# An rwkv7 and convolution block: the channel-tile loop ordered by a list scheduler, full-array chain products, the solve's small steps on GpSimd

## The chip, the cores and the metric

The kernel runs on one core of a Trainium2 chip. Its engines are TensorE (PE, with its weight loads PEld), VectorE (DVE), ScalarE (ACT), GpSimd (POOL) and SyncE (SP, which issues most DMAs). The metric is the device time of one execution in microseconds (us), as the median of three timed runs. A profile of one more execution gives the trace that all rows below come from.

## The reference

One block on 512 tokens and 1024 channels: an rwkv7 time mix and a conformer convolution run side by side on the normed input, are gated and merged, and a gated feed-forward part of width 2816 follows. What matters here is the loop over channel tiles:

```python
def wkv7(r, w, k, v, a, b):          # 16 heads of 64 channels
    def step(S, inp):
        r_t, w_t, k_t, v_t, a_t, b_t = inp
        sa = einsum('bhvk,bhk->bhv', S, a_t)
        S = S * w_t + sa[..., None] * b_t + v_t[..., None] * k_t
        return S, einsum('bhvk,bhk->bhv', S, r_t)
    ...
def conformer_conv(p_c, dw, ...):
    c = u * sigmoid(gate)             # u, gate = halves of p_c
    c = depthwise_conv(c, dw, 31 taps, causal) + dw_b
    return silu(layer_norm(c)) @ w_o
```

Before it stand r, k, v, the decay, a and g as products of the normed input with weights, partly through low-rank factors; behind it a norm per head, the gates and the output projections.

## The kernel before, in words

Channels lie on the partitions, tokens along the free dimension (T = 512). The loop runs over eight channel tiles of 128, that is two heads each. Every large fp32 product is made of three products of 128x512 with halves of the operands (hi by hi, hi by lo, lo by hi: `acc3`, L179 to L181). A weight arrives in fp32 (`wf`) and is split into `wh` and `wl`, by a copy on ScalarE and a subtraction on VectorE (L159, L160), or, for 106 halves inside the loop, by two copies on ScalarE (L168, L169) and an accumulating DMA of GpSimd's queue (L170).

Per tile, `plan_decay` makes the decay's exponentials and two low-rank products (`zw`, `za`, by `low2`, L412 and L413, the second of them over 64 rows); `plan_keys` and `plan_recept` make keys and receptance, each from a dense product `dn`; `plan_inner` makes the masked products inside chunks of 64 tokens (`gps`, L589) and writes the matrices `Mt`, `AR` and `GR`. `plan_solve` inverts (I - M): VectorE transposes `Mt` to `Mo` (L622), takes 31 steps of a product and a sum (`tt`, L634; `Ps`, L638), transposes back (`P`, L647), and small products (`wps` L659, `xps` L670) fill in the block matrix `Pbd`. `plan_values` makes the token-major values `UV` and `SV` (`vps` L695, `bps` L704). `plan_chain` is the recurrence over eight chunks: `zt` from `AR` and the state `SV` (L718), evicted as `zs` (L721), multiplied with `Pbd` (L726), evicted to `UV` (L738), then the state's update (L730 with the identity, L744 with `bkT`), evicted to `SV` (L751), and the outputs `yp` (L763, L759). All of these are 64-wide products, one for each of the two heads, on quarters or halves of the array. `plan_finish` norms the outputs; `plan_conv` runs the 31 taps of the convolution on VectorE (L841, L844).

The order of the program is a table of nominal times. Each piece is put down by `at(ct, t)`, where `ct` is the tile and `t` a position worked out from constants (PERIOD 44, SOLVE 25, CHP 5.5 and so on); at the end the list is sorted and called:

```python
    def at(ct, t):
        def add(fn):
            plan.append((ct * PERIOD + t, len(plan), fn))
...
    for t_, _, fn in sorted(plan, key=lambda e: e[:2]):
        fn()
```

Each engine takes its instructions in the order in which they are written, as far as their semaphores allow. Only taps and solve steps are tied to one another by hand (`order`, with `solved` and `tapped`), as both run on VectorE. Weights are loaded ahead as far as four buffers go (`plan_halves`).

## Time and profile before

| what | value |
| --- | --- |
| timed runs | 1147.42, 1139.44, 1155.11 us; median 1147.42 |
| profiled execution, span | 1165.1 us |
| mean granted TensorE clock over the span | 0.950 |
| busy share of PE, DVE, ACT, POOL | 98%, 62%, 53%, 8% |

The span goes from the first to the last instruction of the profiled execution, which is a little longer than the timed runs: the median of those is 0.985 of it. Sums of durations from the trace are made against the span. The loop of channel tiles lies between about 67 and 575 us, the taps of the last convolution tiles, the output projections and their norms behind it, and the feed-forward part runs from about 805 us to the end.

### The profile page before, as it was taken

To read this page: it belongs to the slowest core of one execution; us is meant where nothing else is said; L and a number is where in the kernel's file an instruction comes from. 1 tells how busy PE (TensorE), PEld (TensorE's weight loads), DVE (VectorE), ACT (ScalarE), POOL (GpSimd) and SP (SyncE) were. 2 spreads that over 40 slices of the span, in tenths; PEclk is the share of its full clock that TensorE was granted. 3 is DMA by queue.
4 is the path that set the end of the run, shared out by engine and by line. 5 is a ranking of instruction groups with operands and counts; after the bars stand their busy time and mean duration, and the time that the engine had idled before them with its cause. 6 is when DMAs were issued, how large, how long until landed. Compare 5 with 4: busy or idle time off the path is not lost.

```text
span 1165.1 us, 17942 instructions
## 1 busy us (share of the span) xinstructions
PE 1138.6 (98%) x6506; PEld 869.8 (75%) x6506; DVE 721.4 (62%) x1699; ACT 616.5 (53%) x1291; POOL 96.2 (8%) x140
## 2 busy tenths in 40 slices
PE   7999999999999999999999999999999999999996
PEld 5777675757676767677788788899888888888886
DVE  7968676747776748699698737546444444433324
ACT  6777776758756747564655724535333333333321
POOL 0111010101010101112222000000000000000000
PEclk9999988869988869899999999999999999999998
DMA  7145342524342423356798434500332322333322
GB/s 245 44 100 118 78 98 46 116 46 92 71 100 50 97 69 81 68 125 147 163 203 197 117 99 139 178 19 10 101 98 91 99 91 94 96 91 109 109 64 73
DMA packets 74202, 117.41 MB, mean 101 GB/s; under 512 B 15745, under 2 KB 21249, under 8 KB 74113
## 3 DMA queue, kind: packets, MB, share of 16 engines
q1 hardware_dynamic: 58848, 88.47, 25.2%
q0 software_dynamic: 15264, 27.79, 14.3%
q8 instruction: 51, 0.84, 0.3%
q14 instruction: 39, 0.31, 0.1%
HBM read 84.25 MB, written 2.10 MB: 74 GB/s over the span
## 4 chain that ended last, share of the span: by engine, by line
PE 91%; ACT 4%; DVE 3%; issue 1%; DMA 0%; SPq 0%; DVEq 0%; ACTq 0%
PE dn L179 22%; PE dn L181 22%; PE dn L180 22%; PE gps L589 3%; PE yp L759 2%; PE zt L726 2%; PE zt L718 2%; PE vps L695 1%; PE zt L744 1%; PE yp L763 1%; PE bps L704 1%; PE ss L194 1%; PE psf L180 1%; PE psf L179 1%; PE psf L181 1%
## 5 line engine op out<-in xcount | busy, mean ns | idle before, releaser
L159 ACT ACTIVATE wh<-wf 128x512 fp32r<-128x512 f32 (+1 forms) x172 | 106.6, 621 | 245.5 <-PE dn L180 237.8
L160 DVE TENSOR_TENSOR wl<-wf,wh 128x512 fp32r<-128x512 f32 (+1 forms) x172 | 116.0, 676 | 136.1 <-ACT wh L159 136.1
L179 PE MATMUL dn<-HH,wh 128*128 128x512 f32 x408 | 173.0, 426 | 0.8 <-DVE cpad L823 0.5
L844 DVE SCALAR_TENSOR_TENSOR ca<-cpad,dw,ca 128x512 f32<-128x512 f32 x240 | 171.8, 744 | 1.4
L180 PE MATMUL dn<-HL,wh 128*128 128x512 f32 x408 | 172.1, 422 | 0.0
L181 PE MATMUL dn<-HH,wl 128*128 128x512 f32 x408 | 171.1, 420 | 0.0
L170 POOL DMA_DIRECT2D wl<-wf x106 | 91.6, 870 | 505.3 <-ACT wl L169 325.6
L181 PE MATMUL dn<-FHH,wl 128*128 128x512 f32 x320 | 127.0, 397 | 0.0
L179 PE MATMUL dn<-FHH,wh 128*128 128x512 f32 x320 | 126.6, 395 | 0.0
L180 PE MATMUL dn<-FHL,wh 128*128 128x512 f32 x320 | 125.8, 393 | 0.0
L168 ACT ACTIVATE wh<-wf 128x512 fp32r<-128x512 f32 x106 | 66.3, 629 | 69.1 <-PE dn L180 68.1
L179 PEld LDWEIGHTS dn<-HH,wh 128*128 128x128 f32 x408 | 78.9, 194 | 18.9 <-issue 0.7
L181 PEld LDWEIGHTS dn<-HH,wl 128*128 128x128 f32 x408 | 78.6, 193 | 17.6 <-issue 0.5
L180 PEld LDWEIGHTS dn<-HL,wh 128*128 128x128 f32 x408 | 79.0, 194 | 16.4 <-issue 0.4
L180 PEld LDWEIGHTS dn<-FHL,wh 128*128 128x128 f32 x320 | 60.2, 188 | 15.0
L181 PEld LDWEIGHTS dn<-FHH,wl 128*128 128x128 f32 x320 | 60.1, 188 | 14.5
L179 PEld LDWEIGHTS dn<-FHH,wh 128*128 128x128 f32 x320 | 60.0, 188 | 13.8
L169 ACT ACTIVATE wl<-wh 128x512 fp32r<-128x512 f32 x106 | 66.3, 628 | 2.1 <-ACT UV L738 0.4
L179 PE MATMUL dn<-FH,wh 128*128 128x512 f32 (+1 forms) x166 | 64.3, 387 | 0.0
L181 PE MATMUL dn<-FH,wl 128*128 128x512 f32 (+1 forms) x166 | 64.1, 386 | 0.0
L180 PE MATMUL dn<-FH,wh 128*128 128x512 f32 (+1 forms) x166 | 64.1, 386 | 0.0
L638 DVE TENSOR_TENSOR Ps<-Ps,tt 128x60 f32<-128x60 f32 (+24 forms) x248 | 52.6, 212 | 3.4
(303 smaller groups left out, 2111.0 us busy)
## 6 DMA issues: line engine op xcount, KB each, us to landing
wf<-in_w_in_dram SPq DMA_DIRECT2D x112, 256.0 KB, 3.1
wl<-wf POOLq DMA_DIRECT2D x106, 256.0 KB, 3.7
wf<-in_w_gt_dram SPq DMA_DIRECT2D x44, 256.0 KB, 2.6
wf<-in_w_up_dram SPq DMA_DIRECT2D x44, 256.0 KB, 2.8
wf<-in_w_dn_dram SPq DMA_DIRECT2D x40, 256.0 KB, 2.7
wf<-in_w_ro_dram SPq DMA_DIRECT2D x16, 256.0 KB, 3.0
wf<-in_w_co_dram SPq DMA_DIRECT2D x16, 256.0 KB, 2.6
wf<-in_w_o_dram SPq DMA_DIRECT2D x16, 256.0 KB, 2.9
```

The costliest lines, as they stand in the source:

```text
L159: S.activation(out=hi, in_=src, func=AF.Copy)
L160: V.tensor_sub(lo, src, f(hi))
L168: S.activation(out=wh, in_=wf, func=AF.Copy)
L169: S.activation(out=wl, in_=f(wh), func=AF.Copy, scale=-1.0)
L170: G.dma_start(out=wl, in_=wf, accum_op=ALU.add)
L179: PE.matmul(ps, lhsT=a, rhs=rh(k), start=first and j == 0, stop=False)
L180: PE.matmul(ps, lhsT=a, rhs=rl(k), start=False, stop=False)
L181: PE.matmul(ps, lhsT=b, rhs=rh(k), start=False, stop=last and j == n - 1)
L589: PE.matmul(ps[:, c, :], lhsT=bk[R, hc * 4 + c, :], rhs=AR[R, hc * 4 + c, par:par + 2, :], start=True, stop=True)
L638: solved[0] = V.tensor_add(Ps[:, 0:j, q0:8], Ps[:, 0:j, q0:8], tt)
L718: PE.matmul(zt[R, 0, :], lhsT=AR[:, c, 2 * par, :], rhs=SV[:, c, par, :], start=True, stop=True)
L844: a_ = V.scalar_tensor_tensor(out=o_, in0=cb[:, j:j + T], scalar=tap(j), in1=o_, op0=ALU.mult, op1=ALU.add)
```

## The change

The table of nominal times goes. In its place each tile's work is written as generators (`prep`, `solve`, `values`, `chain`, `finish`, `taps`), whose calls go to a list scheduler in the source (`Sched`). It holds its own estimate of what every instruction takes (`times`), finds dependencies from the operands' regions, and at each turn takes, among the ready instructions that could start within EPS of the earliest, the one of the best priority: chain 0, loads and the low-rank inputs 1, `prep` and `values` 2, `solve` and `finish` 3, dense products 4, taps 5. Every engine's instructions are then pinned in that order, by a dependency on the last one issued. Lines of these instructions all read L290, the call inside the scheduler; only code outside it keeps its own lines.

Four other things change. The chain step's products become one each over the whole array: `AR` is stored so that both heads' parts stand side by side, `Pbd` is block diagonal and 128 wide, and the identity and `bkT` products take both heads in 128x128; `zs` is evicted in two instructions instead of one, and the outputs `yp` are made four chunks at a time (`outputs`). The second low-rank product takes all 128 rows, with a zero-padded `w2l`. The solve's 62 products and sums per tile go from VectorE (V) to GpSimd (G). The buffers of `Mt` go from 1 to 2, the taps add up in a buffer of their own (`cacc`), and 56 weight halves instead of 106 go through GpSimd's DMA, the others through VectorE's subtraction.

On PE, inside a chain step in the middle of a tile, this stood before (`dn` are dense products, `zt` and `yp` the chain's):

```order
L744 MATMUL zt<-UV,bkT 64x64 x2
L763 MATMUL yp<-GR,UV 64x64 x2
L181 MATMUL dn<-HH,wl 128x512
L179 MATMUL dn<-HH,wh 128x512
L759 MATMUL yp<-AR,SV 64x64
L180 MATMUL dn<-HL,wh 128x512
L718 MATMUL zt<-SV,AR 64x64 x2
L759 MATMUL yp<-AR,SV 64x64
L181 MATMUL dn<-HH,wl 128x512
L179 MATMUL dn<-HH,wh 128x512
L180 MATMUL dn<-HL,wh 128x512
L726 MATMUL zt<-zs,Pbd_484 64x64 x2
```

And now, again from one chain step to the next:

```order
L290 MATMUL zt<-zs,Pbd_513 128x64
L290 MATMUL dn<-HL,wh 128x512
L290 MATMUL dn<-HH,wl 128x512
L290 MATMUL dn<-HH,wh 128x512
L290 MATMUL dn<-HL,wh 128x512
L290 MATMUL zt<-SV,cs 128x128
L290 MATMUL zt<-UV,bkT 128x128
L290 MATMUL dn<-HH,wl 128x512
L290 MATMUL dn<-HH,wh 128x512
L290 MATMUL dn<-HL,wh 128x512
L290 MATMUL dn<-HH,wl 128x512
L290 MATMUL dn<-HH,wh 128x512
```

The pairs of 64x64 products have become single ones of 128x128 or 128x64, the `yp` are gone from between them, and dense products stand between every two.

On DVE, from the transpose `Mo` of one tile on, this stood before (`tt` and `Ps` are the solve, `ca` the taps):

```order
L622 STREAM_TRANSPOSE Mo<-Mt 128x1024
L634 TENSOR_TENSOR tt<-Mo,Ps 128x31
L638 TENSOR_TENSOR Ps<-Ps,tt 128x31
L634 TENSOR_TENSOR tt<-Mo,Ps 128x30
L638 TENSOR_TENSOR Ps<-Ps,tt 128x30
L634 TENSOR_TENSOR tt<-Mo,Ps 128x29
L705 TENSOR_TENSOR ya<-bps,mu_v 128x512
L638 TENSOR_TENSOR Ps<-Ps,tt 128x29
L495 SCALAR_TENSOR_TENSOR cum<-cs,cum 128x512
L634 TENSOR_TENSOR tt<-Mo,Ps 128x28
L531 TENSOR_SCALAR n_3380<-ss 128x8
L638 TENSOR_TENSOR Ps<-Ps,tt 128x28
```

Now the rows ahead of the transpose `P` of the third tile (number 2) are these, where `cacc` and `ca` are taps and products of the convolution:

```order
L290 SCALAR_TENSOR_TENSOR cacc<-ca,dw,cacc 128x512 x2
L290 SCALAR_TENSOR_TENSOR ca<-th,dn 128x512
L290 SCALAR_TENSOR_TENSOR cacc<-ca,dw,cacc 128x512 x2
L290 TENSOR_TENSOR g2l<-g2f,g2h 128x128
L290 SCALAR_TENSOR_TENSOR cacc<-ca,dw,cacc 128x512 x4
L290 SCALAR_TENSOR_TENSOR ca<-ca,dw,cacc 128x512
L290 TENSOR_SCALAR cacc<-ca,dw,pr 128x512
L290 SCALAR_TENSOR_TENSOR cacc<-ca,dw,cacc 128x512 x14
L290 SCALAR_TENSOR_TENSOR mu_v<-dn,pr,mu_v 128x511
L290 SCALAR_TENSOR_TENSOR cacc<-ca,dw,cacc 128x512 x3
L290 STREAM_TRANSPOSE P_1913<-Ps 128x32x8
L290 STREAM_TRANSPOSE P32T<-P_1913 128x256
```

The solve's steps have left VectorE, and taps stand in a row where they used to alternate with them.

On POOL, over some two tiles in the middle of the loop, this stood before (`wl` are the weight DMAs):

```order
L170 DMA wl<-wf 128x512 x6
L701 MEMSET SV 64x64
L702 MEMSET SV 64x64
L498 MEMSET ep 128x8
L170 DMA wl<-wf 128x512 x7
L701 MEMSET SV 64x64
L702 MEMSET SV 64x64
L170 DMA wl<-wf 128x512
L498 MEMSET ep 128x8
L170 DMA wl<-wf 128x512 x8
```

Now the first rows of the third tile's solve read:

```order
L290 DMA wl<-wf 128x512
L290 TENSOR_TENSOR tt<-Mo,Ps 128x31
L290 TENSOR_TENSOR Ps<-Ps,tt 128x31
L290 TENSOR_TENSOR tt<-Mo,Ps 128x30
L290 TENSOR_TENSOR Ps<-Ps,tt 128x30
L290 TENSOR_TENSOR tt<-Mo,Ps 128x29
L290 TENSOR_TENSOR Ps<-Ps,tt 128x29
L290 TENSOR_TENSOR tt<-Mo,Ps 128x28
L290 TENSOR_TENSOR Ps<-Ps,tt 128x28
L290 TENSOR_TENSOR tt<-Mo,Ps 128x54
L290 TENSOR_TENSOR Ps<-Ps,tt 128x27x2
L290 DMA wl<-wf 128x512
```

The solve's chain of products and sums is now GpSimd's, with weight DMAs between its steps, each of which waits for ScalarE's copy of the weight.

The diff, cut to its core ("..." marks what is left out; in the old code, `plan_solve` and `plan_chain` stand above):

```diff
-BUFS = (2, 2, 2, 2, 1, 1, 1)
-# nominal positions that order the program
-PERIOD = 44.0
-NCL = 3
-CPERIOD = 96.0
-CPERIOD2 = 20
-DTZ = 0.25
-CONV0 = 60
-TG_ = 25
+BUFS = (2, 2, 2, 2, 2, 1, 1)
+EPS = 0.15
 WBF = 4
-T0P = 0.0
-T1P = 475
-TE0 = -26.0
-TN0 = -10
-DTC = 0.3
-POST = 8
-TZO = 20
-LEAD = 11
-DTF = 0.9
-SOLVE = 25.0
-CH0 = -2
...
+        LAG = {"PE": 0.06, "ACT": 0.07, "DVE": 0.06, "POOL": 0.1, "SP": 0.1}
...
+            if eng == "PE":
+                lhsT, rhs = k["lhsT"], k["rhs"]
+                n, m = math.prod(rhs.shape[1:]), math.prod(lhsT.shape[1:])
+                if lhsT.dtype == F32R:
+                    c = max(0.112, 0.452e-3 * n)
+                elif name == "transpose":
+                    c = 0.112
+                elif m > 64:
+                    c = 2 * max(0.112, 1.02e-3 * n)
+                else:
+                    c = 0.058 if m > 32 else 0.016
+                return c, c + 0.17, 0.0
...
+            if eng == "POOL":
+                t = 0.2 + (1.0e-3 if len(aps) < 3 else 2.2e-3) * n
+                return t, t, 0.0
...
+        def after(self, d, o, kind):
+            if d.eng == o.eng and not d.land:
+                return 0.0 if kind == 1 or d.eng == "PE" else d.end + 0.03
+            return d.end + self.LAG[d.eng]
...
+        def issue(self, o, s):
+            e, t = o.eng, max(self.clock[o.eng], o.ready)
+            if o.mode is not None:
+                if self.mode not in (None, o.mode):
+                    t += 0.12
+                self.mode = o.mode
+            self.now = max(self.now, t)
+            self.clock[e] = t + o.busy
+            o.end = t + o.took
+            if o.land:
...
+            i = fn(*a, **k)
+            if self.last[e] is not None:
+                order(i, self.last[e])
+            self.last[e] = i
...
+        def feed(self):
+            self.loaded = [u for u in self.loaded if not u[-1].issued]
+            while len(self.loaded) < WB:
+                if not self.halves:
+                    i = next((i for i, e in enumerate(self.items)
+                              if all(n in self.posted for n in e[0])), None)
+                    if i is None:
+                        return
+                    self.halves += self.items.pop(i)[1]()
+                ld, units = self.halves.pop(0)
+                self.cur, self.pri = "load", 1
+                ld(G if self.fast else None)
+                self.cur, self.pri = "dense", 4
+                self.loaded.append([u() for u in units])
...
+                for e in self.ENGS:
+                    heads = [(max(self.clock[e], q[0].ready), q[0], s)
+                             for s, q in self.queues[e].items() if q and not q[0].wait]
+                    if not heads:
+                        continue
+                    t0 = min(h[0] for h in heads) + EPS
+                    t, o, s = min((h for h in heads if h[0] <= t0),
+                                  key=lambda h: (h[1].pri, h[1].seq))
+                    if best is None or t < best[0]:
+                        best = t, o, s
+                if best is None:
+                    break
+                _, o, s = best
+                self.queues[o.eng][s].pop(0)
+                self.issue(o, s)
...
+    V, G, S = Engine("DVE", nc.vector), Engine("POOL", nc.gpsimd), Engine("ACT", nc.scalar)
+    PE, SY = Engine("PE", nc.tensor), Engine("SP", nc.sync)
...
-    def low2(ps, h_, l_, R, X):
+    def low2(ps, h_, l_, X):
         PE.matmul(ps, lhsT=h_, rhs=X, start=True, stop=False)
-        PE.matmul(ps, lhsT=l_[R], rhs=X[R], start=False, stop=True)
+        PE.matmul(ps, lhsT=l_, rhs=X, start=False, stop=True)
...
+    def dense_tile(wap, then, rh=hh, rl=hl, need=(), ev=None):
...
+            if k == NT - 1:
+                sc.pri = 1
+                then(d["ps"])
+                sc.pri = 4
+                if ev:
+                    sc.post(ev)
...
+    def prep(ct):
...
+        for R, c in ((E, slice(0, P)), (O, slice(P, 2 * P))):
+            V.tensor_sub(w2l[R, c], w2f[R, c], f(w2h[R, c]))
...
+    def solve(ct):
         s_ = st[ct]
-
...
+        for j in range(B32 - 1, 0, -1):
             q0 = j // 4
             n = 8 - q0
             tt = kp.tile([P, j, n], F32, tag="tt", bufs=2, name="tt")
-            a_ = V.tensor_mul(tt, Mo[:, j, 0:j].unsqueeze(2).to_broadcast([P, j, n]),
-                              Ps[:, j, q0:8].unsqueeze(1).to_broadcast([P, j, n]))
-            if tapped[0] is not None:
...
-            solved[0] = V.tensor_add(Ps[:, 0:j, q0:8], Ps[:, 0:j, q0:8], tt)
...
+            G.tensor_mul(tt, Mo[:, j, 0:j].unsqueeze(2).to_broadcast([P, j, n]),
+                         Ps[:, j, q0:8].unsqueeze(1).to_broadcast([P, j, n]))
+            G.tensor_add(Ps[:, 0:j, q0:8], Ps[:, 0:j, q0:8], tt)
...
+        pb = Pbd[ct % 2]
+        for h in range(2):
+            for j, R in enumerate((R1[h], R2[h])):
+                S.activation(out=pb[R, :, h * L + j * B32:h * L + (j + 1) * B32], in_=P32[R],
+                             func=AF.Copy)
...
+    def chain(ct):
         s_ = st[ct]
...
+        if ct:
+            yield ("chain", ct - 1)
+        yield ("val", ct)
+        yield ("solve", ct)
+        AR, GR, UV, SV, pb, bkT, dL = (s_[n] for n in ("AR", "GR", "UV", "SV", "pb", "bkT", "dL"))
+        yp = None
+
+        def outputs(cs_):
+            for c in cs_:
+                if c > 0:
+                    for par, R in ((0, E), (1, O)):
+                        PE.matmul(yp[R, c, :], lhsT=SV[R, c, par, :], rhs=AR[R, c, 2, :],
+                                  start=c == 1, stop=False, skip_group_check=True)
+            for c in cs_:
+                for par, R in ((0, E), (1, O)):
+                    PE.matmul(yp[R, c, :], lhsT=UV[:, c, par, :], rhs=GR[:, c, par, :],
+                              start=False, stop=True, skip_group_check=True)
+
+        for c in range(NCH):
+            zt = pc.tile([P, 5, L], F32, tag="ch", name="zt")
+            PE.matmul(zt[:, 0:2, :], lhsT=AR[:, c, 0:2, :], rhs=SV[:, c, :, :],
+                      start=True, stop=True)
+            zs = sp.tile([P, L], F32, tag="zs", name="zs")
             for par, R in ((0, E), (1, O)):
...
+                S.activation(out=zs[R], in_=zt[R, par, :], func=AF.Copy)
+            PE.matmul(zt[:, 2, :], lhsT=pb[:, c, :], rhs=zs, start=True, stop=True)
             for par, R in ((0, E), (1, O)):
...
+                S.activation(out=UV[R, c, par, :], in_=zt[R, 2, :], func=AF.Copy)
             if c < NCH - 1:
+
+                if c > 0:
+                    PE.matmul(zt[:, 3:5, :], lhsT=ident, rhs=SV[:, c, :, :],
+                              start=True, stop=False)
+                PE.matmul(zt[:, 3:5, :], lhsT=bkT[:, c, :], rhs=UV[:, c, :, :],
+                          start=c == 0, stop=True)
                 for par, R in ((0, E), (1, O)):
...
+                    S.activation(out=SV[R, c + 1, par, :], in_=zt[R, 3 + par, :], func=AF.Identity,
                                  scale=dL[R, c:c + 1])
...
+            if c == NCH // 2 - 1:
+                yp = s_["yp"] = py.tile([P, NCH, L], F32, tag="y", name="yp")
+                outputs(range(0, NCH // 2))
+        outputs(range(NCH // 2, NCH))
+        sc.post(("chain", ct))
+        sc.spawn(once(lambda: finish(ct)), 3)
...
+    def taps(ct):
+        tap = lambda j: dw[:, ct * KW + j:ct * KW + j + 1]
+        yield ("cv", ct)
+        if ct:
+            yield ("taps", ct - 1)
         else:
...
+            yield "low1"
+        cb, o_ = conv_in[ct], csum_[:, 0:T]
+        V.tensor_scalar(out=o_, in0=cb[:, 0:T], scalar1=tap(0), scalar2=vec("conv_b", ct),
+                        op0=ALU.mult, op1=ALU.add)
+        for j in range(1, KW):
+            to = o_ if j < KW - 1 else conv_place(ct)[:, KW - 1:]
+            V.scalar_tensor_tensor(out=to, in0=cb[:, j:j + T], scalar=tap(j), in1=o_,
+                                   op0=ALU.mult, op1=ALU.add)
+        sc.post(("taps", ct))
+        if ct == NT - 1:
+            sc.fast = False
...
+        for g_, pri in ((prep, 2), (values, 2), (chain, 0), (taps, 5)):
+            sc.spawn(g_(ct), pri)
```

## Rows read from the trace of the kernel before

**Rows 1.** The page: busy us, share of the span; granted clock in 40 slices.

```profile
PE 1138.6 (98%) x6506; PEld 869.8 (75%) x6506; DVE 721.4 (62%) x1699; ACT 616.5 (53%) x1291; POOL 96.2 (8%) x140
PEclk9999988869988869899999999999999999999998
```

**Rows 2.** Table by stretches (from:to, length, then as its header says).

```profile
core 0: us, PE busy (x) PEld busy (x) DVE busy (x) ACT busy (x) POOL busy (x), PEclk, DMA share, GB/s
67.00:575.00 508.00, 501.44 (x3497) 345.12 (x3496) 357.91 (x1071) 337.39 (x819) 70.62 (x97) 0.89 0.41 89
223.00:286.00 63.00, 62.59 (x415) 41.35 (x415) 39.86 (x131) 41.02 (x101) 6.45 (x10) 0.78 0.32 70
286.00:337.00 51.00, 50.49 (x412) 35.15 (x411) 39.34 (x129) 39.32 (x98) 7.31 (x11) 1.00 0.42 91
...
900.00:1000.00 100.00, 100.00 (x431) 80.59 (x430) 48.06 (x72) 34.15 (x54) 0.00 (x0) 1.00 0.30 95
```

**Rows 3.** The same table for the dense products dn alone.

```profile
67.00:575.00 508.00, 291.50 (x959) 172.40 (x960) 19.77 (x27) 21.48 (x33) 0.89 0.41 89
...
286.00:337.00 51.00, 27.17 (x90) 15.47 (x90) 2.17 (x3) 1.96 (x3) 1.00 0.42 91
```

**Rows 4.** The same table, the loop's six stretches at half clock (one, and all).

```profile
225.40:252.70 27.30, 27.30 (x131) 16.18 (x132) 13.54 (x49) 13.24 (x37) 1.06 (x2) 0.51 0.20 39
...
sum 109.20, PE 109.06 PEld 67.58 DVE 47.91 ACT 54.71 POOL 6.01; mean PE 18.18 PEld 11.26 DVE 7.98 ACT 9.12 POOL 1.00
```

**Rows 5.** Chain of waits, 286 to 300 us: start, us, what.

```profile
289.49 0.86 PE vps L695 x6
290.35 0.27 PE zt L744 x4
290.62 0.12 PE yp L763 x4
...
291.38 0.26 PE yp L759 x2
291.64 0.27 PE zt L718 x4
...
293.00 0.26 PE zt L726 x4
293.27 0.12 PE zt L730 x4
293.38 0.42 PE za L413
...
298.62 0.43 PE dn L181
299.05 0.23 PE dn L179
```

**Rows 6.** By tile: duration ns min/median/max, first and last start.

```profile
L659 PE MATMUL wps<-P32T,Mt x256: 191/191/212, 106.3 to 510.6; 32*32 32x32 f32 x128
L638 DVE TENSOR_TENSOR Ps<-Ps,tt x248: 157/216/243, 80.7 to 506.7; 128x60 f32<-128x60 f32 x12, 128x54 f32<-128x54 f32 x8, 128x66 f32<-128x66 f32 x8, 128x28 f32<-128x28 f32 x8
L622 DVE STREAM_TRANSPOSE Mo<-Mt x8: 1908/1927/1965, 78.5 to 465.3; 128x1024 f32<-128x1024 f32 x8
```

**Rows 7.** GpSimd by line and shape: busy us, mean ns, idle before.

```profile
L170 POOL DMA_DIRECT2D wl<-wf x106 | 91.6, 870 | 505.3 <-ACT wl L169 325.6 <-DVE wg L160 53.3 <-ACT zs L721 21.8
L701 POOL MEMSET SV<- 64x64 f32 x8 | 1.5, 189 | 22.3 <-ACT zs L721 14.3 <-ACT wh L168 8.0
```

**Rows 8.** Chain of waits, 500 to 512 us, at a tile's transposes.

```profile
506.89 1.32 DVE ca L844 x2
508.22 0.62 DVE P L647
```

**Rows 9.** The page, and ScalarE by line: the weight halves.

```profile
L160 DVE TENSOR_TENSOR wl<-wf,wh 128x512 fp32r<-128x512 f32 (+1 forms) x172 | 116.0, 676 | 136.1 <-ACT wh L159 136.1
L169 ACT ACTIVATE wl<-wh 128x512 fp32r<-128x512 f32 x106 | 66.3, 628 | 2.1 <-ACT UV L738 0.4
```

More of the change, by code (lines that the diff above doesn't have):

```diff
@@ L810, in plan_conv, with conv_place, conv @@
+    conv_in = {}
+    def conv_place(ct):
+        if "ca" not in acts:
+            acts["ca"] = hp.tile([P, NT, KW - 1 + T], F32, tag="ca", name="ca")
+            G.memset(acts["ca"][:, :, 0:KW - 1], 0.0)
+        return acts["ca"][:, ct, :]
+    def conv(ct):
         cv = {}
-        t0 = conv_at(ct)
-        cb = cpad[ct % 2]
         def gate(ps):
@@ L886, in _ @@
         mid["YL"] = mp.tile([P, NT, T], F32R, tag="m2", name="YL")
+        sc.post("mid")
+        for m in range(NT):
+            yield ("ya", m)
+            split(act("ya")[:, m, :], mid["YH"][:, m, :], mid["YL"][:, m, :])
+        sc.post("split")
     def gate_c(m, ps):
```

948 lines of the change are left out of this document (517 added, 431 removed).

## The prediction

> **What bounds the kernel now.** The page comes first: TensorE is busy 98% of a span of 1165.1 us, VectorE 62%, ScalarE 53%, GpSimd 8% [rows 1]. A busy TensorE is not one at its peak, so the next view is the table by stretches. In the feed-forward part, 900 to 1000 us, 431 products of 128x512 take 100 us at full clock, 0.232 us each [rows 2]. That is the price of a dense product with nothing in its way, and the reader should hold the loop of channel tiles against it. The loop's body lies between 67 and 575 us: 508 us, of which the dense products are 959 [rows 2, 3]. At 0.232 they are worth 223 us, and 285 us remain, 35.7 us for each of the eight tiles. Tiles follow one another about every 58 us (the product wps, one group per tile, starts at 106.3 in the first and by 510.6 in the last [rows 6]). The stretch 286 to 337, one tile at full clock, takes 51 us with 90 dense products: 51 - 20.9 = 30.1 us beside them [rows 2, 3]. The stretch before it takes 63 us at clock 0.78. So what is to be had lies in the loop, in the 36 us per tile that are no dense products: 109.2 us of the loop pass at 1.2 GHz, in six stretches [rows 4], and within a chain step the change of shapes costs TensorE more than the arithmetic does [rows 5]. Behind 575 the dense products run nearly back to back, and the change leaves their number as it is; I cost that part at nothing.
>
> **Chain step (priced from the chain of waits at full clock).** Before, one step is seven groups of half-array products: zt L718 0.27, yp L763 0.12, yp L759 0.26 twice, zt L726 0.26, zt L730 0.12, zt L744 0.27, together 1.56 us. Each return to a dense product costs it 0.43 where its neighbours have 0.23 [rows 5], and a step has four returns: 1.56 + 4 x 0.19 = 2.32 us. After, a step has AR.SV, Pbd.zs, ident.SV and bkT.UV as one product each, 3.6 on average as the first and last chunk have fewer. Such a product of plain fp32 is in the trace as two passes; vps L695 has six passes of 128x128 in 0.86 us, 0.143 each [rows 5], so 0.29 a product and 1.05 a step. The four yp products of a step, batched four chunks at a time, cost what a group of four passes without a change of shape costs (0.12, zt L730), twice: 0.24. One change of shape per step is 0.26 - 0.12 = 0.14. Sum 1.43, saved 0.89 us in each of 64 steps: **-57 us**. The four evictions of a step become five (zs split in two), on a ScalarE that is 53% busy; they lie on the chain's own path, beside dense products. The second low-rank product goes from 64 rows to 128, so it no longer costs 0.42 (za L413) but 0.23, like any product of that size behind one of its own shape [rows 5]; two per tile and the returns with them: **-5 us**.
>
> **The order from a list scheduler.** By my working the best stretch pays 30.1 us beside the dense products and the average tile 35.7. The scheduler offers a dense product whenever a chain product waits, on every engine at once; I take it that all tiles then cost what the best one does: 8 x 5.6 = **-45 us**. Ends: nothing, if as much time at half clock comes back [rows 4], and about -60 if the best tile is beaten too. Against it stand 64 x 4 hand-offs between TensorE and ScalarE, now placed by a model of the times where they were placed by hand; I estimate 0.1 us each for what the model misses: **+25 us** (0 to 50; the nearest rows are the ends of a dense product, 0.23 us, which is what a late product costs in order).
>
> **The solve on GpSimd.** 62 small products and sums per tile leave VectorE, where they cost 0.21 us each [rows 6], about 100 us in all, and come to GpSimd. No row shows a two-input operation there. Nearest below: VectorE's own 0.21, and GpSimd's memset of 64 columns, 0.189, which reads nothing. Above: the issue of a weight DMA on GpSimd, 0.87 [rows 7]. I take 0.35, about two of the memsets, since it reads two operands and writes one. A tile's solve is then 62 x 0.35 = 21.7 us, plus seven weight DMAs that the order puts between its steps, 7 x 0.87 = 6.1, plus VectorE's transposes Mo 1.93 and P and P32T 0.62 each [rows 6, 8]: 31 us. Its cover is what TensorE has queued between the last masked product gps of a tile and its first wps, which waits for P. In tile 2 these are 93 dense products (21.6 us), 29 chain products (8.3), 30 yp and some norm products: about 34 us by the prices above. Counted the same way the eight tiles have 32.6, 37.9, 33.8, 35.0, 29.2, 34.0, 34.0 and 16.6. So the solve is just covered except in tile 4 (2 us) and the last (14): **+15 us**. What stands behind a late wps is everything on TensorE, since each engine's order is pinned: the dense products too. Each 0.1 us more per step is some 6.2 us per tile, 45 us in all; at VectorE's price the term is about 5, at the DMA's price over 200.
>
> **Costed at nothing.** 50 weight halves go from GpSimd's accumulating DMA to a subtraction on VectorE: 50 x 0.68 = 34 us more there and 50 x 0.63 less on ScalarE [rows 9], while VectorE loses the solve's 100 us; if its cover were gone, 34 us would show. The taps (0.66 us each back to back [rows 8]) all come before the last tile's solve in the new order, where they used to run on to 629 us; the layer norm behind them waits for the output products' turn in either. GpSimd's queue: a weight DMA now stands between solve steps and waits for ScalarE's copy; its buffer is one of four, so a wait of a microsecond holds a solve, which the 31 us above include only as the 0.87 of the issue.
>
> **Sum.** -57 - 5 - 45 + 25 + 15 = -67 us on a span of 1165.1, so 1098. The three timed runs have their median at 1147.42, 0.985 of the span. Forecast: 1098 x 0.985 = **1081 us**, -5.8%. The three runs spread over 1.4%, so about 2% is what a measurement can tell from no change.
>
> **Rivals.** *First, the taps hold the solve (slower).* VectorE and GpSimd now run two-input operations at the same time, which before never happened. The Trainium skill, "SBUF — State Buffer", section "Who interferes with whom", says that a VectorE instruction with two SBUF inputs contends with a GpSimd instruction that reads SBUF, and that the one that comes second is blocked wholly. No row here shows it, since GpSimd read nothing but in DMAs. As a mechanism of this kernel: the order puts 16, 34, 29, 25, 23, 25, 1 and 0 taps on VectorE between a tile's Mo and its P, 153 in all. If a solve step waits out a whole tap each time, 153 x 0.66 = 101 us come on top of solves that have no cover left. 1081 + 0.985 x 101 = **1180 us**. It decides the sign from about half of that wait: the forecast loses its lead of 66 us when a step's mean with its waits passes 0.35 + 66/440 = 0.50 us. For it: the taps stand back to back in those places, and nothing else on GpSimd's path has slack. Against it: only that no trace shows a block. *Second, GpSimd is slow by itself*, 0.6 us a step or more without any tap: + 0.25 x 450 = 113, **1190 us** and above. Memset rows speak against it, the DMA row for it. *Third, the order doesn't do what it says*: half clock stays (no -45, or hand-offs at the upper end): 1081 + 45, **about 1125 us**.
>
> **How the numbers follow.** Forecast with its own range 1040 to 1110: 0.50. Third rival 0.18, first 0.23, second 0.09. The low end is the sum without its two additions, 1165.1 - 107 = 1058, times 0.985: 1042. The upper end must take in most of the first rival: 1190. Faster by over 2% means below 1124.5: the forecast and half of the third with a little of a weak first: 0.62. Within 2%: 0.16. Slower: 0.22.
>
> **What the new profile would show.** Solve steps on GpSimd at 0.35 us start to start, and no longer beside taps than beside an idle VectorE (then the first rival is wrong). wps waiting for P under 3 us per tile but for the last. zt products of 128x128 at 0.29 us with no dense product of 0.43 behind them. Granted clock in the loop near 1. A wait of TensorE for P of 10 us and more in tiles 1 to 5, with taps running through it, is the first rival; the same with VectorE idle is the second. The prediction is wrong by its own terms if dense products beside the chain cost clearly over 0.232 us at full clock.

## The result, and the profile after

The changed kernel takes 1247.08 us (median of four runs, 1244.74 to 1253.8) against 1146.04 before (median of four too): a ratio of 1.0896, 95% interval 1.0821 to 1.0971. The forecast was 1081 with 1190 as its upper end; the sign is wrong, and only the second rival, "1190 us and above", reaches as far, whose condition (0.6 us a step without any tap) is not met below.

The profile of the kernel before (1165.1 us at a granted clock of 0.950) is of an execution some 20 us slower than the median of its timed runs, that of the changed kernel (1243.0 us) is not, so the two profiles differ by 78 us where the timed runs differ by 101.

The page of the changed kernel, answering to [rows 1]: TensorE is busy 90% instead of 98%, GpSimd 21% instead of 8%, and the granted clock is under 0.9 in 14 slices ahead of the last one, up to the 20th of 40, instead of 9.

```profile
PE 1123.8 (90%) x6042; PEld 900.1 (72%) x6042; DVE 709.6 (57%) x1261; ACT 615.8 (50%) x1311; POOL 257.9 (21%) x587
...
PEclk9879898979887887877699999999999999999998
```

The loop now ends near 640 us, where it ended near 575. The table by stretches of the changed kernel (columns as in [rows 2]), first everything, then the dense products alone as in [rows 3]:

```profile
67.00:350.00 283.00, 239.28 (x1407) 185.69 (x1408) 212.29 (x372) 177.10 (x407) 142.79 (x282) 0.88 0.40 87
350.00:640.00 290.00, 240.24 (x1613) 184.98 (x1613) 161.83 (x314) 171.78 (x462) 112.33 (x293) 0.80 0.21 53
```

```profile
67.00:350.00 283.00, 151.33 (x514) 98.51 (x515) 11.60 (x16) 10.95 (x17) 0.88 0.40 87
350.00:640.00 290.00, 120.19 (x373) 69.17 (x373) 8.82 (x12) 8.68 (x13) 0.80 0.21 53
```

573 us hold 887 dense products, where 508 us held 959 [rows 3]. That accounts for the whole difference between the two profiles: 65 us later, with 72 products of 0.232 us still to do, 17 us, makes 82, and the span is 78 us longer. TensorE is idle for 94 of these 573 us, where it was idle for 7 of the 508 [rows 2]. What TensorE waited for in the changed kernel (us in total, times, longest us):

```profile
PE wps L290 <- DVE P32T L290: 24.2, 6, 8.5
PE dn L290 <- DMA wl<-wf: 22.3, 11, 3.4
PE gps L290 <- ACT Mt L290: 8.9, 8, 4.3
```

The first is the solve coming late. The prediction allowed 2 us for it in tile 4 and 14 in the last; it came in tiles 1, 2, 4 and 5, with 4 to 8.5 us each, and with 0.4 in the last. Before, the same wait was this:

```profile
PE wps L659 <- DVE P32T L650: 0.9, 2, 0.5
```

The second is new and was not in the sum: dense products wait for weight halves whose DMA stands behind solve steps in GpSimd's queue. No such wait stands among those of the kernel before.

The solve's steps in the changed kernel, by tile, answering to [rows 6] (ns min/median/max), and its weight DMAs, answering to [rows 7]:

```profile
L290 POOL TENSOR_TENSOR tt<-Mo,Ps x248: 202/296/1082, 99.2 to 589.0; 128x60 f32<-128x60 f32 x12, 128x54 f32<-128x54 f32 x8, 128x66 f32<-128x66 f32 x8, 128x28 f32<-128x28 f32 x8
L290 POOL TENSOR_TENSOR Ps<-Ps,tt x248: 203/319/1562, 99.5 to 589.3; 128x60 f32<-128x60 f32 x12, 128x54 f32<-128x54 f32 x8, 128x66 f32<-128x66 f32 x8, 128x28 f32<-128x28 f32 x8
```

```profile
L290 POOL DMA_DIRECT2D wl<-wf x56 | 50.4, 914 | 103.8 <-ACT wl L290 69.1 <-PE tps L290 15.3 <-PE ss L290 9.7
```

A median of 0.3 us and a maximum of 1.56: the steps come in two kinds. Sorted by what VectorE does at the same time, 219 of the 496 lie beside an operation that reads two operands from SBUF and take 0.62 us on the mean (median 0.67), 226 lie beside nothing at 0.276, and 42 beside an operation with one operand in PSUM at 0.282. From the first step to the last, the solves of tiles 0 to 4 last 36 to 41 us, those of the last two, which have next to no taps beside them, 25 and 24. That is no longer than before, where steps alternated with taps on VectorE and the eight solves lasted 24 to 49 us by the same count: what is new is that TensorE waits for their end.

One place shows the two kinds of steps. Of the chain of waits from 107 us (start, us, what), and VectorE's own row of time beside it:

```profile
107.16 0.30 POOL tt L290
107.46 0.07 issue
107.53 0.88 POOL Ps L290
...
108.48 0.36 POOL tt L290
108.84 0.07 issue
108.91 0.73 POOL Ps L290
...
110.99 1.07 POOL Ps L290
```

```profile
107.53 0.69 DVE L290 TENSOR_TENSOR GL<-lo_f,GH 128x512 fp32r<-128x512 f32 x1 [5.69 <-ACT GH L290]
108.14 0.55 DVE L290 TENSOR_SCALAR cacc<-cpad,dw,pr 128x512 f32<-128x512 f32 x1
108.72 3.94 DVE L290 SCALAR_TENSOR_TENSOR cacc<-cpad,dw,cacc 128x512 f32<-128x512 f32 x5
```

The same `Ps` step that takes 0.3 us takes 0.88 when a two-operand subtraction of 0.69 starts with it, and 0.73 to 1.07 through the five taps.

### The profile page after: what moved, and what is told of

Read it like the earlier page. It is cut to its first block, busy times and chain, and to the rows that moved or that the text cites. A ratio compares the mean times of both kernels' runs of the same rounds, so it can differ in the third digit from the quotient of the medians.

```text
span 1243.0 us, 16932 instructions
## 1 busy us (share of the span) xinstructions
PE 1123.8 (90%) x6042; PEld 900.1 (72%) x6042; DVE 709.6 (57%) x1261; ACT 615.8 (50%) x1311; POOL 257.9 (21%) x587
## 4 chain that ended last, share of the span: by engine, by line
PE 62%; POOL 15%; DVE 11%; issue 6%; ACT 3%; DMA 1%; SPq 0%; POOLq 0%; DVEq 0%; ACTq 0%
PE dn L215 32%; PE dn L290 18%; POOL Ps L290 7%; POOL tt L290 6%; DVE cacc L290 4%; PE gps L290 2%; PE psf L215 2%; PE zt L290 2%; PE wo L215 1%; PE lora L290 1%; POOL wl L290 1%; DMA wl<-wf 1%; DVE AR L290 1%; DVE Mo L290 1%; ACT Mt L290 1%
## 5 line engine op out<-in xcount | busy, mean ns | idle before, releaser
L290 PE MATMUL dn<-HH,wl 128*128 128x512 f32 x408 | 173.8, 426 | 22.3 <-DMA wl<-wf 22.3
L215 ACT ACTIVATE wh<-wf 128x512 fp32r<-128x512 f32 x140 | 86.6, 618 | 216.2 <-PE dn L215 208.7
L290 PE MATMUL dn<-HH,wh 128*128 128x512 f32 x408 | 173.6, 425 | 0.5 <-ACT wh L290 0.5
L290 PE MATMUL dn<-HL,wh 128*128 128x512 f32 x408 | 173.9, 426 | 0.0
L215 DVE TENSOR_TENSOR wl<-wf,wh 128x512 fp32r<-128x512 f32 x140 | 94.2, 674 | 120.6 <-ACT wh L215 120.6
L290 DVE SCALAR_TENSOR_TENSOR cacc<-ca,dw,cacc 128x512 f32<-128x512 f32 x203 | 153.0, 754 | 5.4
L290 POOL TENSOR_TENSOR tt<-Mo,Ps 128x60 f32<-128x60 f32 (+24 forms) x248 | 101.0, 407 | 147.2 <-DVE Mo L290 50.3
L290 ACT ACTIVATE wh<-wf 128x512 fp32r<-128x512 f32 x138 | 86.1, 627 | 83.4 <-PE dn L290 72.0
L290 POOL TENSOR_TENSOR Ps<-Ps,tt 128x60 f32<-128x60 f32 (+24 forms) x248 | 112.5, 454 | 17.9
L290 PEld LDWEIGHTS dn<-HH,wl 128*128 128x128 f32 x408 | 81.1, 199 | 41.0 <-DMA wl<-wf 26.3
L215 PE MATMUL dn<-FH,wh 128*128 128x512 f32 (+1 forms) x332 | 100.8, 386 | 0.0
L290 PEld LDWEIGHTS dn<-HH,wh 128*128 128x128 f32 x408 | 81.8, 201 | 16.0 <-ACT wh L290 1.1
L290 PEld LDWEIGHTS dn<-HL,wh 128*128 128x128 f32 x408 | 81.6, 200 | 15.6 <-issue 1.0
L290 DVE TENSOR_TENSOR wl<-wf,wh 128x512 fp32r<-128x512 f32 x82 | 56.1, 688 | 63.8 <-ACT wh L290 60.5
L290 POOL DMA_DIRECT2D wl<-wf x56 | 50.4, 914 | 103.8 <-ACT wl L290 69.1
L215 PEld LDWEIGHTS dn<-FH,wh 128*128 128x128 f32 x332 | 61.5, 188 | 13.3
```

What stands on the lines that cost most here:

```text
L215: return fn(*a, **k)
L290: i = fn(*a, **k)
```

## Experiments

Ratios are to the kernel before on the same chip at the same time; 1% is some 11.5 us.

**e1, the solve back on VectorE.** Only these two lines differ, and the order that follows:

```diff
-            G.tensor_mul(tt, Mo[:, j, 0:j].unsqueeze(2).to_broadcast([P, j, n]),
+            V.tensor_mul(tt, Mo[:, j, 0:j].unsqueeze(2).to_broadcast([P, j, n]),
...
-            G.tensor_add(Ps[:, 0:j, q0:8], Ps[:, 0:j, q0:8], tt)
+            V.tensor_add(Ps[:, 0:j, q0:8], Ps[:, 0:j, q0:8], tt)
```

> The changed kernel with the solve's 62 steps per tile put back on VectorE and planned there; all else as changed. Theory (taps and splits on VectorE hold the solve's steps on GpSimd, which read SBUF too; and the weight DMAs stand behind them in GpSimd's queue): the steps cost 0.21 us again, a tile's solve some 25 us, TensorE's waits for P32T (24 us) and for the weight DMAs (22 us) go, with the low clock that they bring: 1130 to 1175 us. Rival (the scheduler's order or the new chain costs the time, wherever the solve runs): 1215 us or more.

Measured: 1210.88 us, ratio 1.0585 (1.0516 to 1.0653). The solves are 15 to 18 us long but for one of 26, and the wait for P32T falls to 9.2 us. Yet only 36 of the 101 lost us come back: neither the theory's range nor the rival's bound is met, and two thirds of the loss stay with the solve on VectorE. The dense products of e1 (same table) show where to look:

```profile
67.00:350.00 283.00, 163.83 (x579) 109.49 (x579) 12.64 (x18) 11.61 (x18) 0.92 0.44 96
350.00:610.00 260.00, 97.31 (x311) 58.52 (x310) 7.79 (x11) 8.08 (x12) 0.76 0.28 65
```

579 dense products in the first 283 us, 311 in the next 260. The kernel before has 475 and then 484 in 225 us:

```profile
67.00:350.00 283.00, 145.14 (x475) 84.31 (x475) 12.53 (x17) 11.39 (x17) 0.89 0.38 82
350.00:575.00 225.00, 146.36 (x484) 88.08 (x485) 7.23 (x10) 10.08 (x16) 0.89 0.45 97
```

**e2, taps that read one operand.**

```diff
-            V.scalar_tensor_tensor(out=to, in0=cb[:, j:j + T], scalar=tap(j), in1=o_,
-                                   op0=ALU.mult, op1=ALU.add)
+            V.tensor_scalar(out=to, in0=cb[:, j:j + T], scalar1=tap(j), scalar2=tap(j),
+                            op0=ALU.mult, op1=ALU.add)
```

> The changed kernel with each tap but the first made as a product and sum with two scalars, so that it reads one operand from SBUF and not two; the sum over the taps is left out, the count of the instructions stays. They take 0.54 us each instead of 0.75 and VectorE stays busy in the same places. Theory (two operands from SBUF on VectorE hold a GpSimd step that reads SBUF): the median step beside a tap falls from 0.67 to about 0.29 us, the solves of tiles 0 to 4 from 36 to 41 us to about 29, and the time to 1180 to 1210. Rival (any work on VectorE slows GpSimd, or GpSimd is slow by itself): steps beside a tap stay above 0.5 us and the time above 1225.

Measured: 1216.85 us, ratio 1.0632 (1.0588 to 1.0676). Inconclusive: the 102 steps that lie beside such a tap alone take 0.53 us on the mean, so the stand-in (0.55 us itself) holds them nearly as well as the tap does. "Two operands" is not the whole rule; e9 settles which operations hold a step, e13 what the hold costs here.

**e3, no weight DMAs on GpSimd.** `ld(G if self.fast else None)` becomes `ld(None)`.

> The changed kernel with the 56 weight halves of GpSimd's DMA queue split on VectorE instead, as all others are. Theory (the DMAs stand in the solve's chain, 0.91 us each and up to seven in a solve, and dense products wait 22 us for them): no wait for them, solves some 4 us shorter where VectorE has no more two-input work beside them, 1205 to 1230. Rival (the 56 subtractions are two-input operations on VectorE too, and hold as many steps as the DMAs cost): within 1% of 1247.

Measured: 1236.15 us, ratio 1.0806 (1.0763 to 1.0849), just beyond the theory's range and inside the rival's. The wait for weights is gone, the one for P32T has grown from 24.2 to 52.3 us:

```profile
PE wps L290 <- DVE P32T L290: 52.3, 8, 9.3
```

263 steps now lie beside two-operand work (219 before), since the subtractions are such work too. But the solves are not longer: they last 28 to 34 us, 253 in all where it was 273. So the longer wait is not the hold's alone; that TensorE, with no weights to wait for, comes to `wps` earlier would explain it, which is not shown.

**e4, the scheduler told the real price.**

```diff
-                t = 0.2 + (1.0e-3 if len(aps) < 3 else 2.2e-3) * n
+                t = 0.2 + (1.0e-3 if len(aps) < 3 else 2.2e-3) * n + (0.0 if len(aps) < 3 else 0.27)
```

> The changed kernel where the scheduler's own price of a two-operand step on GpSimd is 0.27 us higher, about what the trace shows on the mean beside taps; nothing else is edited, only the order that follows from it. Theory (the loss is that the order was made for solves of 22 us, and TensorE has other work that could stand there): 1200 to 1225. Rival (a late solve is late wherever its wait stands, since the chain of the tile needs it): within 1.5% of 1247.

Measured: 1248.75 us, ratio 1.0919 (1.0874 to 1.0965): the rival. The wait at wps goes, but the solves grow to 45 to 52 us in tiles 0 to 4, since the scheduler puts more taps and DMAs beside steps that it believes slow, and TensorE waits in other places.

**e5 and e6, the convolution's dense products held back,** with the solve on VectorE (e5, from e1) and on GpSimd (e6, from the changed kernel):

```diff
         need = ("low1",) if ct else ()
+        if ct:
+            need += (("keys", min(2 * ct, NT - 1)),)
```

> The kernel with the solve back on VectorE (e1), and the convolution's dense products held back: those of tile ct (1 to 7) may start only when the keys of tile min(2 ct, 7) are made. Theory (the list scheduler gives dense products away as early as they are ready, 104 to 151 per 50 us before 350 us and 24 to 72 per 50 us behind 400, so that the last tiles' chains have nothing to run beside and TensorE waits there at a low clock): the last tiles keep their dense products, no stretch of the loop with under 50 of them per 50 us, 1130 to 1170 us. Rival (the new chain's own latency or the hand-offs between engines set the tile's time, not what runs beside it): 1195 us or more.

> The same hold on the convolution's dense products in the changed kernel itself, with the solve on GpSimd. Theory (two separate losses: the dense products given away early, and the solve held by taps): better than the changed kernel by about as much as e5 is better than e1, 1165 to 1205 us, with the steps beside two-operand work on VectorE still near 0.6 us. Rival (with taps moved to the last tiles the held solves are later than before): 1230 us or more.

Measured: e5 1235.89 us, ratio 1.0786 (1.0731 to 1.0841); e6 1254.71, ratio 1.0961 (1.0898 to 1.1025). e5 is slower than e1, e6 not faster than the changed kernel; the theory falls. e5 does spread the dense products (326 in the first 283 us, 476 in the next 265), and TensorE then waits for the next tile's keys instead, mostly in the early tiles:

```profile
PE tps L290 <- ACT bk L290: 18.3, 3, 6.1
PE ss L290 <- ACT kkn L290: 11.0, 4, 4.0
PE bck L290 <- ACT kkn L290: 11.0, 4, 3.0
```

From one transpose Mo to the next it is 64 us per tile, as in e1, with little else to run in the early tiles. That speaks for dense products given away early being a symptom: a tile's own round takes over 60 us, and the dense products only fill it. e10 tries it.

**e7, the chain step alone,** in the kernel before with its table of nominal times (the core of it; AR, Pbd and the outputs as in the change's diff):

```diff
-            for par, R in ((0, E), (1, O)):
-                PE.matmul(zt[R, 0, :], lhsT=AR[:, c, 2 * par, :], rhs=SV[:, c, par, :],
-                          start=True, stop=True)
+            PE.matmul(zt[:, 0:2, :], lhsT=AR[:, c, 0:2, :], rhs=SV[:, c, :, :],
+                      start=True, stop=True)
```

> The kernel before, with its table of nominal times, where only the chain step is changed: one product over the whole array each for AR.SV, Pbd.zs, ident.SV and bkT.UV, zs evicted in two instructions, the outputs made four chunks at a time. Prediction's term (0.89 us of TensorE's time saved in each of 64 steps): 1090 to 1115 us. Rival (what TensorE saves is waited for elsewhere, since a step's length is set by the evictions between its products): 1130 to 1160 us.

Measured: 1126.01 us, ratio 0.9828 (0.977 to 0.9886). Faster, by 1.1 to 2.3%, below the rival's range and short of the theory's. It is the only version that beats both kernels. Its clock in 40 slices:

```profile
PEclk9999999999999999999999999999999999999998
```

Its dense products in the loop, which ends near 523 us (columns as above):

```profile
67.00:350.00 283.00, 151.42 (x510) 88.19 (x509) 13.29 (x18) 12.84 (x19) 1.00 0.40 85
350.00:523.00 173.00, 118.37 (x435) 76.72 (x434) 6.49 (x9) 8.71 (x14) 1.00 0.53 116
```

**e8, the solve's steps alone on GpSimd,** in the kernel before (V to G in both lines, and the manual order between taps and steps, which now run on different engines, left out):

> The kernel before, with its table of nominal times, where only the solve's 62 steps per tile go to GpSimd. Theory (steps beside two-operand work on VectorE take about 0.6 us, alone 0.28, and all weight halves of the loop pass through the same queue): solves of 30 to 45 us against 24 to 38 before, 1160 to 1200 us. Rival (VectorE's relief makes up for it): within 1.5% of the kernel before.

Measured: 1255.35 us, ratio 1.0999 (1.0861 to 1.1136), worse than the theory's range and about as slow as the whole change. Solves last 26 to 40 us, not the reason by themselves, since the eight lasted 24 to 49 before (the expectation's 38 is too low). The largest new waits are VectorE's and, behind it, ScalarE's (us in total, times, longest us):

```profile
DVE P L645 <- POOL Ps L636: 96.3, 8, 17.1
ACT Pbd L664 <- DVE P L645: 75.0, 6, 16.8
```

VectorE, which no longer has the steps, comes to the transpose `P` early and stands at it. The hand-written order puts the copies to `Pbd` where the solve used to be done; ScalarE stands at them, and behind them in its queue stand the evictions of the tile before, whose chain is still running.

**e9, the disputed cost by itself.** A chain of 40 steps of 128x60 on GpSimd beside 24 operations of one kind on VectorE, stage by stage; the reference's work is left out.

> The reference's work is left out: stages one after another, in each a chain of 40 steps of 128x60 on GpSimd (product and sum, as the solve's) beside 24 operations of 128x512 of one kind on VectorE: none; a tap with both operands in SBUF; a tap with one of them in PSUM; a product and sum with two scalars held in SBUF; the same with constants; the same from PSUM; a copy; a difference of two SBUF operands; a transpose. Theory (an operation on VectorE that reads two operands from SBUF holds GpSimd's step): 0.28 us a step beside nothing, PSUM operands and transposes, 0.6 to 0.7 beside taps and differences. Open: product and sum with two scalars from SBUF, beside which the steps of e2 took 0.53; if it is the scalars from SBUF that count, those with constants let the steps pass at 0.28. Rival (any busy VectorE slows GpSimd): all stages but the first above 0.45.

Measured: each row is 10 us inside a stage, in the order of the expectation without the last stage; the columns that matter are VectorE's and GpSimd's busy time with the number of instructions.

```profile
core 0: us, DVE busy (x) ACT busy (x) POOL busy (x), PEclk, DMA share, GB/s
7.00:17.00 10.00, 0.00 (x0) 0.00 (x0) 7.96 (x27) 1.00 0.00 0
22.00:32.00 10.00, 9.57 (x13) 0.00 (x0) 8.98 (x14) 1.00 0.00 0
47.00:57.00 10.00, 9.54 (x14) 0.00 (x0) 8.04 (x26) 1.00 0.00 1
66.00:76.00 10.00, 9.38 (x18) 0.00 (x0) 8.65 (x18) 1.00 0.00 0
86.00:96.00 10.00, 9.17 (x23) 0.00 (x0) 8.28 (x23) 1.00 0.00 1
105.00:115.00 10.00, 9.56 (x13) 0.00 (x0) 7.96 (x27) 1.00 0.00 0
125.00:135.00 10.00, 9.24 (x23) 0.00 (x0) 8.36 (x22) 1.00 0.00 0
145.00:155.00 10.00, 9.52 (x15) 0.00 (x0) 8.90 (x15) 1.00 0.00 1
```

Read the two counts of a row together. 27 steps pass in 10 us beside nothing, 26 beside taps with one operand in PSUM, 27 beside a product and sum from PSUM. Beside work from SBUF to SBUF the two engines go in lockstep, one step to one operation: 14 to 13 taps, 18 to 18 with two scalars, 23 to 23 with constants, 22 to 23 copies, 15 to 15 differences. Mean steps are 0.31 us alone, 0.69 beside taps, 0.63 beside differences, 0.50 and 0.38 beside product and sum with scalars and with constants. Beside transposes they are 0.31 too, though these go from SBUF to SBUF. The theory holds for two operands and fails as a full rule; the rival falls.

**e10, keys first** (from e1): dense products for keys, receptance and values get a stream of their own.

```diff
-                self.cur, self.pri = "dense", 4
+                self.cur, self.pri = ("keyed", 3) if key else ("dense", 4)
```

> The kernel with the solve back on VectorE (e1), where the dense products for keys, receptance and values go before those of the convolution (a stream of their own at priority 3 instead of 4). Theory (in the new program the keys of a tile wait until those of the tile before are done, and then behind the convolution's dense products; this round, some 62 us per tile, sets the loop's time, whatever runs beside it): some 5 us less per tile, 1150 to 1185 us. Rival (the low clock and waits that no order by these prices avoids): 1200 us or more.

Measured: 1162.75 us, ratio 1.0124 (1.0073 to 1.0174), 48 us less than e1 and within 2% of the kernel before. The theory's range. The tiles follow one another every 54 us instead of 64, and the last chain ends at 552 us instead of 606. Its dense products:

```profile
67.00:350.00 283.00, 170.14 (x584) 108.15 (x584) 13.50 (x19) 11.86 (x18) 0.93 0.48 104
350.00:555.00 205.00, 94.61 (x294) 54.28 (x294) 6.65 (x9) 7.30 (x11) 0.82 0.33 73
```

**e11, keys first with the solve on GpSimd,** and **e12, e10 with another tie width** (`EPS = 0.05`):

> The changed kernel, solve on GpSimd, with the dense products for keys, receptance and values ahead of the convolution's (as e10). Theory (two losses that add up: the order of the dense products, and the steps that VectorE holds on GpSimd): 1162.75 us and some 30 to 50 more, 1190 to 1215, with steps beside SBUF-to-SBUF work on VectorE at 0.5 us or more. Rival (with the better order the solves have cover again): under 1180.

> e10 with the scheduler's tie width EPS at 0.05 us instead of 0.15, and no other edit. By the scheduler's own prices TensorE's last product of the ordered part then ends at 730 us instead of 674. Theory (the measured time follows the order that the rules happen to give, and a greedy order swings by several per cent with a rule that has nothing to do with the hardware): 1200 to 1235 us. Rival (the times on the chip even such differences out): within 1% of 1162.75.

Measured: e11 1229.83 us, ratio 1.0739 (1.068 to 1.0798), 67 us more than e10 and more than expected, and only some 17 less than the changed kernel. The solves are back at 35 to 44 us in tiles 0 to 5, and the shared queue now costs most:

```profile
PE dn L290 <- DMA wl<-wf: 40.1, 17, 8.1
```

e12 1235.04 us, ratio 1.0779 (1.073 to 1.0828), the theory's upper end: 72 us from one constant, 56 by the scheduler's own prices. The trace shows what it did. By these prices a solve step on VectorE is ready 0.11 us after VectorE can take the next instruction (0.08 in `times`, 0.03 in `after`): within a tie width of 0.15, but not of 0.05. So taps, which have the lowest priority, now go between two steps:

```profile
244.18 0.74 DVE L290 SCALAR_TENSOR_TENSOR cacc<-ca,dw,cacc 128x512 f32<-128x512 f32 x1
244.85 0.22 DVE L290 TENSOR_TENSOR Ps<-Ps,tt 128x69 f32<-128x69 f32 x1
244.99 0.74 DVE L290 SCALAR_TENSOR_TENSOR cacc<-ca,dw,cacc 128x512 f32<-128x512 f32 x1
245.65 0.22 DVE L290 TENSOR_TENSOR tt<-Mo,Ps 128x66 f32<-128x66 f32 x1
```

The solves of tiles 0 to 3 last 54 to 59 us, where those of e10 last 20 to 26. That all of the 72 us come from there was not tested.

**e13, taps that let the steps pass** (from the changed kernel), and **e14, e8 without weight DMAs on GpSimd.** They go into what e2 and e8 leave open.

```diff
-            V.scalar_tensor_tensor(out=to, in0=cb[:, j:j + T], scalar=tap(j), in1=o_,
-                                   op0=ALU.mult, op1=ALU.add)
+            V.transpose(out=to, in_=cb[:, j:j + T])
```

> The changed kernel where each tap but the first is a transpose of 128x512 on VectorE, beside which steps on GpSimd pass unhindered (0.31 us in e9) and which takes about as long as a tap (0.71 against 0.75); the sum over the taps is left out, the scheduler prices it as the tap. Theory (the taps hold the steps): the steps beside SBUF-to-SBUF work fall from 219 to under 100, those beside transposes take 0.3 us, the solves of tiles 0 to 4 go from 36 to 41 us to 26 to 31, and the time to 1190 to 1220. Rival (the weight DMAs and splits hold the solves anyway): solves above 33 us and 1230 or more.

> The kernel before with the solve on GpSimd (e8), and the 106 weight halves of GpSimd's queue split on VectorE instead. Theory (in the hand-written order the queue is the larger part of the loss: solve steps wait behind DMAs that wait for ScalarE, and what follows on GpSimd waits behind the steps): 1185 to 1220 us. Rival (the hold by VectorE's work is the loss, and 106 subtractions more hold more steps): 1250 or more.

Measured: e13 1198.53 us, ratio 1.0459 (1.0363 to 1.0555), in the theory's range. The 174 steps beside transposes alone take 0.33 us on the mean, 89 steps are left beside two-operand work, solves of tiles 0 to 4 last 27 to 33 us, and TensorE's wait is down to a third:

```profile
PE wps L290 <- DVE P32T L290: 7.9, 7, 2.4
```

e14 1257.39 us, ratio 1.0971 (1.0893 to 1.1048): the same as e8, the rival's time though not its reason, since the solves are as short as 24 to 29 us. So neither the queue by itself nor long solves explain it. What the trace shows is the place of what follows the solve on in-order engines: VectorE waits 101.3 us for the last steps, in eight places, and ScalarE 70.7 for `P`, in six. That place was not moved by itself.

## Why the prediction was wrong

**The parts, in one chain of ratios.** The chain step alone 0.9828 (e7). With the list scheduler around it, the solve still on VectorE, 1.0585 (e1): the order adds 7.7%, some 85 us; the wider low-rank product, the second `Mt` buffer and the 50 moved weight halves are in that too and were not run apart. With the solve on GpSimd 1.0896: another 2.9%, 36 us. The three give -20, +85 and +36, which is the measured +101. They hold in this chain only, since the parts act on one another: the solve on GpSimd costs 36 us here, 67 with keys first (e11 against e10) and some 10% in the order of before (e8), and the rule of e10 gives 48 us with the solve on VectorE, some 17 with it on GpSimd.

**The order from the list scheduler: the step that failed.** The prediction took it that all tiles would cost what the best one did, -45, with +25 for hand-offs. It read the best stretch of the old order as something that a scheduler reaches by itself. Measured, +85 stands where these two sum to -20: 105 of the 166 us by which the forecast missed. Shown by e10: 48 us of it are one rule, that the dense products a tile's own round depends on stand in one queue with the convolution's, which nobody waits for. In the changed kernel the keys of a tile may start only when those of the tile before are done, and then wait behind weights and products already fed; this round is 64 us in e1, and 64 in e5, which has other work beside it. e12 shows how easily such an order goes wrong: its tie width lets taps go before solve steps, and 72 us are lost. What is left between e10 and e7, some 3%, shows in rows: TensorE is busy 20 of the 32 us from 67 to 99 in the changed kernel at a granted clock of 0.63, with no dense product among its work, as the next tile's keys are held by rule until the first one's are made; and e10's 294 dense products in its last 205 us against e7's 435 in 173. Neither was tried by itself.

**The chain step: the sign right by luck, the mechanism not.** -57 was forecast, -20 measured alone. Start to start at full clock, the chain's 928 half-array `zt` passes of before take 0.057 us each and its 480 `yp` passes 0.079: 91 us. In e7 464 full-array `zt` passes take 0.129 and 480 `yp` passes 0.066: 92 us. So TensorE's time in the chain is the same; a full-array product costs what two half-array ones cost, and the changes of shape that were to go moved to the batched `yp`. Dense products take 0.241 us on the mean in both, so the returns did not go either. Of the 0.89 us a step that the prediction counted, TensorE saves nothing. What e7 has instead is the clock: 10 us of its profile at 1.2 GHz against 119 before. The runs before come out some 20 us below their profile at the median, so the timed gain is smaller than the 47 us between the two profiles. The four runs of before behind the ratio have a granted clock of 0.962 to 0.972, those of e7 0.988 to 0.996. As an estimate from these (the share that was not granted, times the run), the clock costs them at most some 36 and 10 us, a difference that covers the 20. Why the clock stays up in e7 is open.

**The solve on GpSimd: priced right alone, not beside VectorE.** 0.35 us a step was taken, start to start, with 0.50 as the point where the sign turns. Alone the steps last 0.28 us here (0.31 in e9) and the next starts 0.08 later, so 0.35 is what was taken. The mean of all 496 is 0.43 (213.6 us in all), or 0.51 from start to start, just past the point named. By the prediction's 45 us for each 0.1, (0.51 - 0.35) x 450 = 72 us should come on top of its +15; e1 measures 36 in all, so that price was too high here. e13 shows that the taps are the cause: with stand-ins that let steps pass, nearly the same order is 49 us faster, and faster than e1 too (with the sum over the taps left out). The first rival named the mechanism, with 101 us for what e13 measures as 49; its 1180 fails because it stood on the sum of the other terms. The Trainium skill, "SBUF — State Buffer", section "Who interferes with whom", has a VectorE instruction with two SBUF inputs contend with a GpSimd one that reads SBUF: the trace agrees (0.62 against 0.28 us).

**Costed at nothing.** The weight DMAs between solve steps were not nothing: dense products wait 22.3 us for them, 40.1 in e11. The prediction saw the DMA holding the solve and not the solve holding the DMA. That the taps finish before the last solve was true (the last tap of the loop starts at 510 us, the last solve at 563); that it gained anything is not shown.

**The clock.** Time at 1.2 GHz in each profile, summed over its stretches, of which about 10 us lie at the very end: e7 10 us, before 119, e10 134, e11 170, e13 171, e2 and e14 174, e1 190, the changed kernel 201, e8 202, e3 208, e6 213, e12 214, e5 220, e4 231. The versions with the list scheduler leave TensorE idle for longer in the loop than before (31 us in e10, 63 in e1, 94 in the changed kernel, against 7, from the same tables for all of PE) and have more of it. Idle time alone does not set it, though: e7 has 13 us idle in its loop and none at 1.2 GHz, before 7 and 109. What lowers the clock stays open. A slower clock lengthens what follows: from one dense product to the next it is 0.233 us at full clock and 0.427 at half in the changed kernel (medians). So at most half of such time is lost to the clock, and between the two profiles, 201 against 119, that is at most 41 of the 78 us. It is part of each number above, and nothing was run that changes the clock alone. The rest of e8's 10% stays open too: the waits for `P` were not moved.

## What to carry to other kernels

A list scheduler is worth what its rules know: give the products that the next tile's round depends on their own priority, and don't take a good stretch of the old order as its forecast. Look in the trace at what its constants do: a tie width can decide whether a tap goes before a solve step. Before work goes to an idle engine, ask what its neighbour does at that very time, and price the step beside that work, not alone; 0.28 us became 0.62 here. And before a wider product is booked as a gain, compare passes start to start, not groups of a chain; and when a version is faster, look whether its engine does less or its clock is higher.

## What the runs showed of the hardware

A GpSimd step that reads SBUF and a VectorE operation from SBUF to SBUF take turns, one for one, even when the VectorE operation has one operand: 18 and 18 in 10 us with two scalars in SBUF, 23 and 22 with a copy. With its operand in PSUM, or as a transpose, they don't. The Trainium skill, in the section named above, says that with at most one SBUF input and outside the 2-port modes there is no contention; the product and sum with two scalars takes 0.55 us for 512 columns, where those with constants take 0.43, and holds the steps all the same. Whether it runs in such a mode is not shown here.

A pass of a full-array plain fp32 product of 128x128 costs TensorE about as much as two half-array ones (0.129 us start to start on the mean in e7 against 0.057 before, with waits and changes of shape in both).
